# A chunk-by-chunk order for the first fresh tiles, and Newton steps on two columns at once

## The chip, the cores and the metric

The kernel runs on one core of a Trainium2 chip. Its time is the device time of one execution in microseconds (us); the number quoted is the median of three runs. A profile is one further execution with a hardware trace. TensorE (PE) multiplies matrices, VectorE (DVE) and ScalarE (ACT) work element by element, GpSimd (POOL) helps a little, and SyncE's queue (SP) loads weights from memory.

## What is computed

Two network blocks in a row, for 256 tokens of width 1024, in float32. The first block is an RMS norm, two recurrent mixers, and a mixture of 32 experts. The second block has two layers, each of which treats the tokens `h` and, beside them, 256 context tokens `hc`: a feed-forward, a mixer of two attentions and a Fourier branch, and a second feed-forward. The change touches the norms of both blocks and the feed-forwards and mixers of the second. Cut to these:

```python
def rmsnorm_2(x, g):
    return x * lax.rsqrt(jnp.mean(x * x, axis=-1, keepdims=True) + EPS) * g

def swiglu(x, wi, wo):
    g, u = jnp.split(x @ wi, 2, axis=-1)        # 1024 -> 2 x 2816
    return (jax.nn.silu(g) * u) @ wo            # 2816 -> 1024

def ffn_half(h, m, k, g_norm, wi, wo):
    hn = modulate(rmsnorm_2(h, g_norm), m[3 * k], m[3 * k + 1])   # * (1 + scale) + shift
    return h + 0.5 * m[3 * k + 2][:, None, :] * swiglu(hn, wi, wo)

for l in range(2):                              # second block
    h = ffn_half(h, ml, 0, ...); hc = ffn_half(hc, mc, 0, ...)
    hn = modulate(rmsnorm_2(h, norm_g[l, 1]), ml[3], ml[4])
    qa, ka, va, qb, kb, vb, uc, gl = project_tokens(hn, w_in[l], ...)
    h = h + ml[5][:, None, :] * merge_branches(ya, yb, yc, gl, ...)   # attentions and Fourier
    h = ffn_half(h, ml, 2, ...)
```

## The kernel before

Activations lie transposed: a tile of 128 features by 256 tokens, eight such chunks (k = 0 to 7) for the width of 1024. A product of full float32 quality is made of three matmuls (`mm3`, L327 to L329): both the weights and the activations are split in a high half (`whi`, `hnh`) and a low half (`wlo`, `hnl`), and high by high, low activation by high weight, and high activation by low weight are added up in one PSUM bank. So every output tile of 128 features costs 8 x 3 matmuls.

Weights come in pieces of 128 x 1024, that is eight 128 x 128 blocks. Class `_Stream` loads them in order, and splits each just before its first use: ScalarE writes `whi` (L312), VectorE subtracts and writes `wlo` (L313). There are three buffers for the halves in the second block, so piece c can be split only when TensorE has finished with piece c - 3. Here a piece is what one output tile needs: piece c holds the eight blocks of tile c.

Work is arranged in chains. Chain x is the first block's recurrent mixers, m the experts, c the context tokens, and z the main tokens in the second block; x, m and z follow each other, and c runs between x's and m's work, steered by a planner with estimated costs. A chain is a Python generator that issues instructions as it goes. TensorE and the SP queue keep the order in which the instructions were issued; on VectorE, ScalarE and GpSimd the framework's scheduler sets the order at build time, from its own estimates. On the chip every engine works its list off in that order, and a waiting instruction holds up all that stand behind it.

A norm goes like this (`rstd_cols`, L409): ones-matmuls (L421) leave the mean square of each token in a PSUM bank as two columns of 128 tokens; VectorE makes 1/sqrt of them by a bit trick (L423 to L426) and three Newton steps; two diagonal matrices `dg` (L442) and two matmuls (L443) spread the result over all partitions. Then `norm_split` writes the eight chunks of `hnh` and `hnl` (L456 to L462). The helper `rsqrt` (L342 to L344) makes the same Newton steps for the head norms with three instructions on all columns. There are 14 norms of the kind `rstd_cols`: x and m one each, c five, z seven.

In chain z the norms of the feed-forwards and mixers need not be awaited: `norm_early` runs the first six output tiles (pieces 0 to 5) on the raw activations `xs0`, `xs1`, and VectorE scales their results afterwards by `hnr` (L398, L399). These tiles are j < 3 of a feed-forward (each j is a gate tile and an up tile, two pieces) and j < 6 of a mixer. The first fresh tiles, which read `hnh` and `hnl`, come next: j = 3 of the feed-forward (pieces 6 and 7, in `up`, L1532) and j = 6 and 7 of the mixer (`project`, L1579). Chain c has no early tiles: its first fresh tiles are j = 0, and they already go chunk by chunk, so that a chunk of `hn` can be used as soon as it is there.

Of the kernel before, what the change touches and what calls it, by code (L numbers as in the profile page):

```python
# [15 lines left out]
OP = mybir.AluOpType  # L16
# [3 lines left out]
T = 256  # L20
D = 1024
KD = D // 128
# [201 lines left out]
class _Net:  # L224
# [184 lines left out]
    def rstd_cols(self, ch, x, w1=0.7, w2=2.2):  # L409

        nc, V = self.nc, self.nc.vector
        have = ch.top.acc is not None
        if not have:
            for k in range(KD):
                self.sumsq(ch, x[:, k], k, eng=V)
        acc, ch.top.acc = ch.top.acc, None
        yield 0.0, w1 if have else 5.0
        b = ch.bank()
        for i in range(2):
            for n, a in enumerate(acc):  # L420
                nc.tensor.matmul(b[:, i:i + 1], a[:, i * 128:i * 128 + 128], self.ones[:, :1], start=(n == 0), stop=(n == 1))  # L421
        v, a, y, t = (ch.tile([128, 2], f"rs{c}", bufs=2) for c in "vayt")
        V.tensor_scalar(v, b[:, :2], 1.0 / D, EPS, op0=OP.mult, op1=OP.add)  # L423
        V.tensor_scalar(t.bitcast(I32), v.bitcast(I32), 1, None, op0=OP.arith_shift_right)
        V.tensor_scalar(y.bitcast(I32), t.bitcast(I32), -1.0, float(0x5F3759DF), op0=OP.mult, op1=OP.add)
        V.tensor_scalar(a, v, -0.5, None, op0=OP.mult)  # L426
        c = [slice(i, i + 1) for i in range(2)]
        for _ in range(3):
            for i in c:
                V.scalar_tensor_tensor(t[:, i], y[:, i], a[:, i], y[:, i], op0=OP.mult, op1=OP.mult)  # L430
            for i in c:
                V.scalar_tensor_tensor(y[:, i], t[:, i], 1.5, y[:, i], op0=OP.add, op1=OP.mult)  # L432
        yield 0.5, w2
        return y

# [1082 lines left out]
    def ffn_body(self, ch, x, hn, gate, wi, wo, more, first, nxt):  # L1518
        nc = self.nc
        nh = JF // 2  # L1520

        def early(hi, lo, j):
            (g, gs), (u, us) = (self.scaled(ch, b, first[1]) for b in first[0][2 * j:2 * j + 2])
            nc.scalar.activation(g, g, AF.Identity, bias=gs)
            th = ch.tile([128, T], "w", bufs=ch.nw)
            nc.scalar.activation(th, g, AF.Tanh, scale=0.5)
            nc.vector.scalar_tensor_tensor(g, th, 1.0, g, op0=OP.add, op1=OP.mult)
            nc.vector.scalar_tensor_tensor(u, u, us, g, op0=OP.add, op1=OP.mult)
            nc.scalar.mul(hi, u, 0.5)
            nc.vector.scalar_tensor_tensor(lo, u, 0.5, hi.bitcast(F32), op0=OP.mult, op1=OP.subtract)  # L1530

        def up(p):  # L1532
            hh = ch.tile([128, nh, T], "h0", F32R, bufs=self.nh)
            hl = ch.tile([128, nh, T], "h1", F32R, bufs=self.nh)
            for jj in range(nh):
                j = p * nh + jj
                if first and j < 3:
                    early(hh[:, jj], hl[:, jj], j)
                    continue
                b = ch.bank()  # L1540
                order = [(h, k) for h in range(2) for k in range(KD)]
                for n, (h, k) in enumerate(sorted(order, key=lambda e: e[1]) if j == 0 else order):
                    if self.fine and n and n % 4 == 0:
                        yield 1.3
                    self.mm3(b[:, h * T:h * T + T], wi.get(j * 16 + h * 8 + k), (hn[0][:, k], hn[1][:, k]),
                             k == 0 and (h == 0 or j > 0), k == KD - 1, skip_group_check=(j == 0))
                th = ch.tile([128, T], "w", bufs=ch.nw)
                nc.scalar.activation(th, b[:, :T], AF.Tanh, scale=0.5)
                q = ch.tile([128, T], "w", bufs=ch.nw)
                nc.vector.scalar_tensor_tensor(q, th, 1.0, b[:, :T], op0=OP.add, op1=OP.mult)  # L1550
                hf = ch.tile([128, T], "w", bufs=ch.nw)
                nc.vector.scalar_tensor_tensor(hf, q, 0.5, b[:, T:], op0=OP.mult, op1=OP.mult)
                self.split_act(hh[:, jj], hl[:, jj], hf)
                yield 1.3 if self.fine else 5.2
            return hh, hl

        def down(p, h):
            for jo in range(KD):
                b = ch.bank()
                for k in range(nh):  # L1560
                    self.mm3(b[:, :T], wo.get(p * KD * nh + jo * nh + k), (h[0][:, k], h[1][:, k]), k == 0, k == nh - 1)
                nc.vector.scalar_tensor_tensor(x[:, jo], b[:, :T], gate[:, jo:jo + 1], x[:, jo],  # L1562
                                               op0=OP.mult, op1=OP.add)
                if p == 1 and more:
                    self.sumsq(ch, x[:, jo], jo, nxt)
                yield 3.6

        if self.nh == 2:
            h = []
            for p in range(2):  # L1570
                h.append((yield from up(p)))
            for p in range(2):
                yield from down(p, h[p])
        else:
            for p in range(2):
                h = yield from up(p)
                yield from down(p, h)

    def project(self, ch, hn, l, rope, y, w, first, full=True):  # L1579
# [8 lines left out]
        todo = list(range(18)) if full else [4, 5, 6, 7, 12, 13]  # L1588
        norm = [t for t in todo if t < 13]
        sb = ch.bank()  # L1590
        late = []
        for j in todo:
            if j == todo[0] and not first:
                two = [ch.bank() for _ in range(2)]
                for k in range(KD):
                    for n in range(2):
                        self.mm3(two[n][:, :T], w.get(todo[n] * 8 + k), (hn[0][:, k], hn[1][:, k]), k == 0, k == KD - 1)
            if first and j < 6:
                t, sft = self.scaled(ch, first[0][j], first[1])
                nc.scalar.activation(qk[:, j], t, AF.Identity, bias=sft)  # L1600
                b = qk[:, j]
            elif j in todo[:2]:
                b = two[todo.index(j)]
            else:
                b = ch.bank()
                for k in range(KD):
                    self.mm3(b[:, :T], w.get(j * 8 + k), (hn[0][:, k], hn[1][:, k]), k == 0, k == KD - 1)
            if len(late) == 3 or j > 12:
                for f in late:
                    f()  # L1610
                late = []
            if j < 13:
                sq = ch.tile([128, T], "w", bufs=ch.nw)
                nc.scalar.square(sq, b[:, :T])
                if not first or j >= 6:
                    nc.vector.tensor_copy(qk[:, j], b[:, :T])
                g = j % 4
                mine = [t for t in norm if t % 4 == g]
                late.append(partial(mm, sb[32 * g:32 * g + 32, :T], self.c("sel")[:, (j // 4) * 32:(j // 4) * 32 + 32],
                                    sq, start=(j == mine[0]), stop=(j == mine[-1])))  # L1620
                if j == norm[-1] and not full:
                    for f in late:
                        f()
                    late = []
                    rs = self.parted(ch, self.rsqrt(ch, sb[:, :T], T, EPS, tag="rw"))
            elif j == 13:
                if full:
                    rs = self.parted(ch, self.rsqrt(ch, sb[:, :T], T, EPS, tag="rw"))
                nc.vector.tensor_copy(vaT, b[:, :T])
            else:  # L1630
                lo, hi = uc[:, j - 14, :128], uc[:, j - 14, 128:]
                nc.scalar.copy(hi, b[:, 128:T])
                nc.vector.tensor_tensor(lo, b[:, :128], hi, op=OP.add)
                nc.vector.tensor_tensor(hi, b[:, :128], hi, op=OP.subtract)
            if not first or j >= 6:
                yield 2.7
        fill = _chain(self.values(ch, hn, w, vaT, r), self.fourier(ch, uc, y) if full else None)
        for c in self.rotate(ch, qk, norm, rs, l):
            yield c
            c = next(fill, None)  # L1640
# [552 lines left out]
```

## Time and profile before

| | us |
|---|---|
| median of three runs | 2859.76 (2856.36, 2860.39, 2859.76) |
| profiled execution, its own time | 2842.6 |
| its span from first to last instruction | 2840.8 |
| TensorE busy | 2700.0 |
| VectorE busy | 1781.4 |
| ScalarE busy | 1229.9 |

The profiled execution was 17 us shorter than the median of the runs, and its span is 1.8 us shorter than its own time. Main chain z fills the span from about 1541 us to the end; the first 1500 us hold the first block and the context chain. In the rows below, "x2" joins two instructions of one kind: the duration is then from the start of the first to the end of the second. A bracket at the end of a row is the idle time of that engine just before, and what ended it. A trailing letter in a name is the chain (bz, hnhz: chain z).

### The profile page before, as it was taken

How to read it: one execution, taken by the hardware profiler on the slowest of the kernel's cores; microseconds unless marked ns; L12 is line 12 of the kernel's file. 1: busy time of each engine (PE TensorE's matmuls, PEld its weight loads, DVE VectorE, ACT ScalarE, POOL GpSimd, SP SyncE). 2: the span in 40 equal slices, each digit the busy share in tenths (PEclk: the TensorE clock that was granted, in tenths of full speed). 3: DMA queues.
4: the chain of work that ended last, by engine and by line, in shares of the span. 5: the costliest groups of instructions: out<-in, count | busy, mean ns of one | idle time of the engine just before them, and what ended most of it. 6: DMA issues, size and time to landing. Idle time of an engine off the chain costs nothing. (4 is left out here: it accounts for less than half of the span.)

```text
span 2840.8 us, 59032 instructions
## 1 busy us (share of the span) xinstructions
PE 2700.0 (95%) x24390; PEld 2396.4 (84%) x24390; DVE 1781.4 (63%) x3501; ACT 1229.9 (43%) x2071; POOL 180.7 (6%) x187
## 2 busy tenths in 40 slices
PE   8998879999999999999997999999999999999999
PEld 6765568898677888888886999799999999799999
DVE  4776366455545554555456767777866767777765
ACT  4331143343344443334343545365544545465543
POOL 0110020000000200000000000101100000101100
PEclk9998979999999999999998999999999999999999
DMA  9857777887698889889794555434555555434553
GB/s 339 289 193 268 248 256 272 324 314 257 243 336 321 272 342 355 322 294 375 286 360 179 184 193 198 151 111 142 169 195 193 181 195 200 142 108 148 169 195 127
DMA packets 194562, 670.82 MB, mean 236 GB/s; under 512 B 29170, under 2 KB 33522, under 8 KB 193650
## 3 DMA queue, kind: packets, MB, share of 16 engines
q1 hardware_dynamic: 183856, 659.12, 65.6%
q10 hardware_dynamic: 10434, 7.90, 1.0%
q8 instruction: 192, 3.15, 0.4%
q14 instruction: 80, 0.66, 0.1%
HBM read 657.73 MB, written 5.80 MB: 234 GB/s over the span
## 5 line engine op out<-in xcount | busy, mean ns | idle before, releaser
L313 DVE TENSOR_TENSOR wlo<-raw,whi 128x1024 fp32r<-128x1024 f32 x631 | 775.5, 1230 | 513.1 <-ACT whi L312 499.4
L312 ACT CAST whi<-raw 128x1024 fp32r<-128x1024 f32 x639 | 670.9, 1050 | 763.4 <-issue 262.6
L327 PE MATMUL bz<-hnhz,whi 128*128 128x256 f32 x1920 | 541.8, 282 | 3.5 <-ACT whi L312 2.8
L329 PE MATMUL bz<-hnhz,wlo 128*128 128x256 f32 x1920 | 534.8, 279 | 7.0 <-DVE wlo L313 7.0
L328 PE MATMUL bz<-hnlz,whi 128*128 128x256 f32 x1920 | 534.9, 279 | 4.2 <-DVE hnlz L322 4.2
L327 PE MATMUL bc<-hnhc,whi 128*128 128x256 f32 x1504 | 434.0, 289 | 11.9 <-DMA raw<-win 7.1
L328 PE MATMUL bc<-hnlc,whi 128*128 128x256 f32 x1504 | 422.4, 281 | 6.4 <-DVE hnlc L462 4.7
L329 PE MATMUL bc<-hnhc,wlo 128*128 128x256 f32 x1504 | 421.3, 280 | 4.7 <-DVE wlo L313 4.7
L327 PEld LDWEIGHTS bz<-hnhz,whi 128*128 128x128 f32 x1920 | 363.6, 189 | 13.0 <-issue 6.1
L329 PEld LDWEIGHTS bz<-hnhz,wlo 128*128 128x128 f32 x1920 | 363.9, 190 | 7.7 <-DVE wlo L313 7.7
L328 PEld LDWEIGHTS bz<-hnlz,whi 128*128 128x128 f32 x1920 | 363.6, 189 | 5.5 <-DVE hnlz L322 5.4
L327 PEld LDWEIGHTS bc<-hnhc,whi 128*128 128x128 f32 x1504 | 286.2, 190 | 52.0 <-issue 28.7
L328 PEld LDWEIGHTS bc<-hnlc,whi 128*128 128x128 f32 x1504 | 285.8, 190 | 9.4 <-DVE hnlc L462 7.7
L329 PEld LDWEIGHTS bc<-hnhc,wlo 128*128 128x128 f32 x1504 | 285.7, 190 | 6.5 <-DVE wlo L313 6.5
L327 PE MATMUL bz<-h0z,whi 128*128 128x256 f32 x704 | 194.3, 276 | 0.0
L328 PE MATMUL bz<-h1z,whi 128*128 128x256 f32 x704 | 194.3, 276 | 0.0
L329 PE MATMUL bz<-h0z,wlo 128*128 128x256 f32 x704 | 194.3, 276 | 0.0
L327 PE MATMUL bc<-h0c,whi 128*128 128x256 f32 x528 | 151.4, 287 | 0.0
L328 PE MATMUL bc<-h1c,whi 128*128 128x256 f32 x528 | 146.9, 278 | 0.0
L329 PE MATMUL bc<-h0c,wlo 128*128 128x256 f32 x528 | 146.8, 278 | 0.0
L329 PEld LDWEIGHTS bz<-h0z,wlo 128*128 128x128 f32 x704 | 132.2, 188 | 0.0
L328 PEld LDWEIGHTS bz<-h1z,whi 128*128 128x128 f32 x704 | 132.2, 188 | 0.0
(698 smaller groups left out, 4992.0 us busy)
## 6 DMA issues: line engine op xcount, KB each, us to landing
raw<-wi SPq DMA_DIRECT2D x266, 512.0 KB, 4.7
raw<-moe_gu SPq DMA_DIRECT2D x177, 512.0 KB, 7.7
raw<-wada SPq DMA_DIRECT2D x144, 512.0 KB, 5.8
raw<-wo SPq DMA_DIRECT2D x129, 512.0 KB, 4.3
raw<-wbr SPq DMA_DIRECT2D x108, 512.0 KB, 4.1
raw<-win SPq DMA_DIRECT2D x104, 512.0 KB, 5.5
raw<-moe_dn SPq DMA_DIRECT2D x103, 512.0 KB, 6.8
room<-moe_gu SPq DMA_DIRECT2D x79, 512.0 KB, 9.2
```

What stands on the lines that cost most here:

```text
L312: self.nc.scalar.copy(hi, src)
L313: eng.tensor_tensor(lo, src, hi.bitcast(F32), op=OP.subtract)
L327: mm(out, w[0], x[0], start=first, stop=False, **kw)
L328: mm(out, w[0], x[1], start=False, stop=False, **kw)
L329: mm(out, w[1], x[0], start=False, stop=last, **kw)
```

## The change

Three edits. In `rstd_cols`, each Newton step was four instructions on single columns (two columns, each t = y*a*y and then y = (t + 1.5)*y); now it is three instructions on both columns (t = y*y, t = t*a, y = (t + 1.5)*y), as in `rsqrt`. In `up`, the chunk-by-chunk order was kept for j = 0; now it also holds for j = 3 where the first three were made early: for each k the gate block and the up block are used. In `project`, tiles 6 and 7 are now made together, chunk by chunk, where the first six were made early.

```diff
--- before.py
+++ after.py
@@ -424,12 +424,10 @@
         V.tensor_scalar(t.bitcast(I32), v.bitcast(I32), 1, None, op0=OP.arith_shift_right)
         V.tensor_scalar(y.bitcast(I32), t.bitcast(I32), -1.0, float(0x5F3759DF), op0=OP.mult, op1=OP.add)
         V.tensor_scalar(a, v, -0.5, None, op0=OP.mult)
-        c = [slice(i, i + 1) for i in range(2)]
         for _ in range(3):
-            for i in c:
-                V.scalar_tensor_tensor(t[:, i], y[:, i], a[:, i], y[:, i], op0=OP.mult, op1=OP.mult)
-            for i in c:
-                V.scalar_tensor_tensor(y[:, i], t[:, i], 1.5, y[:, i], op0=OP.add, op1=OP.mult)
+            V.tensor_tensor(t, y, y, op=OP.mult)
+            V.tensor_tensor(t, t, a, op=OP.mult)
+            V.scalar_tensor_tensor(y, t, 1.5, y, op0=OP.add, op1=OP.mult)
         yield 0.5, w2
         return y
 
@@ -1539,11 +1537,12 @@
                     continue
                 b = ch.bank()
                 order = [(h, k) for h in range(2) for k in range(KD)]
-                for n, (h, k) in enumerate(sorted(order, key=lambda e: e[1]) if j == 0 else order):
+                fresh = j == (3 if first else 0)
+                for n, (h, k) in enumerate(sorted(order, key=lambda e: e[1]) if fresh else order):
                     if self.fine and n and n % 4 == 0:
                         yield 1.3
                     self.mm3(b[:, h * T:h * T + T], wi.get(j * 16 + h * 8 + k), (hn[0][:, k], hn[1][:, k]),
-                             k == 0 and (h == 0 or j > 0), k == KD - 1, skip_group_check=(j == 0))
+                             k == 0 and (h == 0 or not fresh), k == KD - 1, skip_group_check=fresh)
                 th = ch.tile([128, T], "w", bufs=ch.nw)
                 nc.scalar.activation(th, b[:, :T], AF.Tanh, scale=0.5)
                 q = ch.tile([128, T], "w", bufs=ch.nw)
@@ -1589,18 +1588,19 @@
         norm = [t for t in todo if t < 13]
         sb = ch.bank()
         late = []
+        ahead = [6, 7] if first else todo[:2]
         for j in todo:
-            if j == todo[0] and not first:
+            if j == ahead[0]:
                 two = [ch.bank() for _ in range(2)]
                 for k in range(KD):
                     for n in range(2):
-                        self.mm3(two[n][:, :T], w.get(todo[n] * 8 + k), (hn[0][:, k], hn[1][:, k]), k == 0, k == KD - 1)
+                        self.mm3(two[n][:, :T], w.get(ahead[n] * 8 + k), (hn[0][:, k], hn[1][:, k]), k == 0, k == KD - 1)
             if first and j < 6:
                 t, sft = self.scaled(ch, first[0][j], first[1])
                 nc.scalar.activation(qk[:, j], t, AF.Identity, bias=sft)
                 b = qk[:, j]
-            elif j in todo[:2]:
-                b = two[todo.index(j)]
+            elif j in ahead:
+                b = two[ahead.index(j)]
             else:
                 b = ch.bank()
                 for k in range(KD):
```

First, TensorE at the first fresh tile of chain z's second feed-forward. The first row is k = 0. `whi_23967` is piece 6, before:

```order
L327 MATMUL bz_23964<-hnhz_23738,whi_23967 128x256
L328 MATMUL bz_23964<-hnlz_23739,whi_23967 128x256
L329 MATMUL bz_23964<-hnhz_23738,wlo_23968 128x256
L327 MATMUL bz_23964<-hnhz_23738,whi_23967 128x256
L328 MATMUL bz_23964<-hnlz_23739,whi_23967 128x256
L329 MATMUL bz_23964<-hnhz_23738,wlo_23968 128x256
```

and after, where `whi_23934` is piece 6 and `whi_23943` is piece 7:

```order
L327 MATMUL bz_23931<-hnhz_23705,whi_23934 128x256
L328 MATMUL bz_23931<-hnlz_23706,whi_23934 128x256
L329 MATMUL bz_23931<-hnhz_23705,wlo_23935 128x256
L327 MATMUL bz_23931<-hnhz_23705,whi_23943 128x256
L328 MATMUL bz_23931<-hnlz_23706,whi_23943 128x256
L329 MATMUL bz_23931<-hnhz_23705,wlo_23944 128x256
```

Before, all 24 matmuls on piece 6 came first, and piece 7 (`whi_23997`) followed. Now the sixth matmul needs `wlo` of piece 7, and pieces 6 and 7 are both in use until the tile's last chunk.

Second, VectorE at the same place, from `wlo` of piece 6 to `wlo` of piece 7, before:

```order
L313 TENSOR_TENSOR wlo_23968<-raw_23965,whi_23967 128x1024
L1527 SCALAR_TENSOR_TENSOR wz_23934<-wz_23943,wz_23934 128x256
L399 TENSOR_TENSOR wz_23949<-bz_23852,hnrz_23672 128x256
L1528 SCALAR_TENSOR_TENSOR wz_23938<-wz_23938,sftz_23939,wz_23934 128x256
L398 COPY sftz_23954<-bz_23883 128x1
L399 TENSOR_TENSOR wz_23953<-bz_23883,hnrz_23672 128x256
L313 TENSOR_TENSOR wlo_23998<-raw_23995,whi_23997 128x1024
```

and after:

```order
L313 TENSOR_TENSOR wlo_23935<-raw_23932,whi_23934 128x1024
L1525 SCALAR_TENSOR_TENSOR wz_23901<-wz_23910,wz_23901 128x256
L399 TENSOR_TENSOR wz_23916<-bz_23819,hnrz_23642 128x256
L1526 SCALAR_TENSOR_TENSOR wz_23905<-wz_23905,sftz_23906,wz_23901 128x256
L398 COPY sftz_23921<-bz_23850 128x1
L399 TENSOR_TENSOR wz_23920<-bz_23850,hnrz_23642 128x256
L313 TENSOR_TENSOR wlo_23944<-raw_23941,whi_23943 128x1024
```

The names are other numbers of the same buffers: nothing moved here. `wlo` of piece 7 still stands behind the scaling of early tile 5 (L399, reading the last early bank).

Third, VectorE at the plain norm with which chain z begins, where the context chain's last head norm (`wc`) is mixed in. From the last bit-trick instruction on, before:

```order
L425 TENSOR_SCALAR rsyz<-rstz 128x2
L343 TENSOR_TENSOR wc<-wc 128x256
L430 SCALAR_TENSOR_TENSOR rstz<-rsyz,rsaz 128x1
L344 SCALAR_TENSOR_TENSOR wc<-wc 128x256
L430 SCALAR_TENSOR_TENSOR rstz<-rsyz,rsaz 128x1
L342 TENSOR_TENSOR wc<-wc 128x256
L432 SCALAR_TENSOR_TENSOR rsyz<-rstz,rsyz 128x1 x2
L343 TENSOR_TENSOR wc<-wc 128x256
L430 SCALAR_TENSOR_TENSOR rstz<-rsyz,rsaz 128x1
L344 SCALAR_TENSOR_TENSOR wc<-wc 128x256
L430 SCALAR_TENSOR_TENSOR rstz<-rsyz,rsaz 128x1
L342 TENSOR_TENSOR wc<-wc 128x256
```

and after:

```order
L425 TENSOR_SCALAR rsyz<-rstz 128x2
L343 TENSOR_TENSOR wc<-wc 128x256
L428 TENSOR_TENSOR rstz<-rsyz 128x2
L344 SCALAR_TENSOR_TENSOR wc<-wc 128x256
L429 TENSOR_TENSOR rstz<-rstz,rsaz 128x2
L342 TENSOR_TENSOR wc<-wc 128x256
L430 SCALAR_TENSOR_TENSOR rsyz<-rstz,rsyz 128x2
L343 TENSOR_TENSOR wc<-wc 128x256
L428 TENSOR_TENSOR rstz<-rsyz 128x2
L313 TENSOR_TENSOR wlo<-raw,whi 128x1024
L344 SCALAR_TENSOR_TENSOR wc<-wc 128x256
L429 TENSOR_TENSOR rstz<-rstz,rsaz 128x2
```

Twelve Newton instructions became nine (six and five of them are in the rows shown). A `wlo` of the context chain, which before stood behind `dgz`, now stands in the second Newton step.

## Rows read from the trace of the kernel before

**Rows 1.** The page, part 1: busy us and share of TensorE.

```profile
PE 2700.0 (95%) x24390; PEld 2396.4 (84%) x24390; DVE 1781.4 (63%) x3501; ACT 1229.9 (43%) x2071; POOL 180.7 (6%) x187
```

**Rows 2.** Waits of TensorE, whole span: waited for: us, times, longest us.

```profile
PE bz L443 <- DVE dgz L442: 9.9, 9, 3.5
...
PE bz L329 <- DVE wlo L313: 7.0, 3, 2.6
...
PE bc L443 <- DVE dgc L442: 5.5, 4, 2.3
```

**Rows 3.** Timeline of VectorE, one norm (start us, duration us, instruction).

```profile
1571.16 0.35 DVE L430 SCALAR_TENSOR_TENSOR rstz<-rsyz,rsaz 128x1 f32<-128x1 f32 x2
...
1571.62 0.34 DVE L430 SCALAR_TENSOR_TENSOR rstz<-rsyz,rsaz 128x1 f32<-128x1 f32 x2
...
1572.53 0.47 DVE L442 TENSOR_SCALAR dgz<-const,rsyz 128x128 f32<-128x128 f32 x2
```

**Rows 4.** Timeline of VectorE, the head norms' helper.

```profile
912.85 0.17 DVE L342 TENSOR_TENSOR rbtc<-rbyc 128x8 f32<-128x8 f32 x1
...
913.45 0.17 DVE L342 TENSOR_TENSOR rbtc<-rbyc 128x8 f32<-128x8 f32 x1
```

**Rows 5.** Timeline of VectorE and TensorE, the norm before the first mixer.

```profile
1757.92 0.16 DVE L398 COPY sftz<-bz 128x1 f32<-128x1 f32 x1 [0.52 <-PE bz L329]
...
1758.51 0.48 DVE L442 TENSOR_SCALAR dgz<-const,rsyz 128x128 f32<-128x128 f32 x2
...
1758.85 0.71 PE L443 MATMUL bz<-dgz,const 128*128 128x128 f32 x4 [1.04 <-DVE dgz L442]
```

**Rows 6.** Timeline of VectorE, ScalarE, TensorE, the plain norm.

```profile
1543.17 0.43 DVE L343 TENSOR_TENSOR wc<-wc 128x256 f32<-128x256 f32 x1
...
1547.99 0.47 DVE L442 TENSOR_SCALAR dgz<-const,rsyz 128x128 f32<-128x128 f32 x2
...
1544.71 1.05 ACT L312 CAST whi<-raw 128x1024 fp32r<-128x1024 f32 x1 [4.51 <-PE bc L328]
...
1548.32 1.22 PE L443 MATMUL bz<-dgz,const 128*128 128x128 f32 x4 [3.52 <-DVE dgz L442]
```

**Rows 7.** Timeline, the main chain's second feed-forward: TensorE, VectorE, ScalarE.

```profile
2038.27 0.29 PE L327 MATMUL bz<-hnhz,whi 128*128 128x256 f32 x1
...
2038.85 0.28 PE L329 MATMUL bz<-hnhz,wlo 128*128 128x256 f32 x1
...
2036.60 1.21 DVE L313 TENSOR_TENSOR wlo<-raw,whi 128x1024 fp32r<-128x1024 f32 x1
...
2038.87 0.41 DVE L399 TENSOR_TENSOR wz<-bz,hnrz 128x256 f32<-128x256 f32 x1
2039.20 1.21 DVE L313 TENSOR_TENSOR wlo<-raw,whi 128x1024 fp32r<-128x1024 f32 x1
...
2035.73 1.04 ACT L312 CAST whi<-raw 128x1024 fp32r<-128x1024 f32 x1
...
2041.09 1.05 ACT L312 CAST whi<-raw 128x1024 fp32r<-128x1024 f32 x1 [0.52 <-PE bz L328]
```

**Rows 8.** Timeline, the main chain's first feed-forward: TensorE, VectorE.

```profile
1590.08 0.39 PE L329 MATMUL bz<-hnhz,wlo 128*128 128x256 f32 x1 [1.88 <-DVE wlo L313]
...
1588.81 1.22 DVE L313 TENSOR_TENSOR wlo<-raw,whi 128x1024 fp32r<-128x1024 f32 x1
...
1590.62 1.22 DVE L313 TENSOR_TENSOR wlo<-raw,whi 128x1024 fp32r<-128x1024 f32 x1
```

**Rows 9.** Timeline, the first mixer's first fresh tile: VectorE, TensorE.

```profile
1772.05 1.23 DVE L313 TENSOR_TENSOR wlo<-raw,whi 128x1024 fp32r<-128x1024 f32 x1
...
1774.42 0.38 PE L327 MATMUL bz<-hnhz,whi 128*128 128x256 f32 x1
```

**Rows 10.** Windows: stretch, length, TensorE busy (count), granted clock, DMA share, GB/s.

```profile
1590.00:1592.00 2.00, 1.92 (x16) 1.00 0.41 127
1995.00:1997.00 2.00, 1.85 (x8) 0.50 0.53 164
```

## The prediction

> **What bounds the kernel now.** I read the page's busy times first. TensorE is busy 2700 of 2840.8 us [rows 1], so the kernel is bound by TensorE and a change in time must come out of its 140 us of gaps, or add to them. Next I read what those gaps waited for [rows 2]. The `dg` matrices that follow the Newton steps account for 9.9 us in chain z and 5.5 in chain c; a part of the 9.9 (two of the nine waits) belongs to the attention's own norm, which the change leaves alone. Waits for `wlo` account for 7.0 us in z, in three waits. In z no fresh tile of a feed-forward or mixer waits for `hnh` or `hnl`: the view has no such row (the waits for `hnlz` there are all at L322, the mixer's output split). The six early tiles last long enough for all eight chunks of `hn` to be ready when the first fresh tile starts. So the wait that a chunk-by-chunk order could shorten is not there, and I looked instead at what the new orders make TensorE need sooner. After 1541 us z's TensorE has nothing else to do in a gap, so what it waits there moves the end by the same amount.
>
> **Newton steps.** Before, the steps of one norm start at 1571.16 and `dg` starts at 1572.53: 1.37 us for 12 instructions, 0.46 us per step (the second step starts at 1571.62) [rows 3]. Two instructions on separate columns overlap: a pair lasts 0.35 us from its first start to its last end, yet a step of two such pairs takes 0.46 us and not 0.70. The new form is one chain: each of the three needs the one just before. The helper for the head norms has this form on 8 columns, and there a step of three instructions takes 913.45 - 912.85 = 0.60 us, 0.20 us for each [rows 4]. So nine of them take 1.80 us and the norm becomes 0.43 us longer, though it issues fewer instructions. Bounds from the rows: if an instruction cost what it does on average before (1.37/12 = 0.114 us), nine would take 1.03 us, 0.34 less than before; if each took as long as a pair does now, half of 0.46, they would take 2.07, 0.70 more. I take 0.20, since that row is the same operations in the same dependence, and only 6 columns wider.
>
> The Trainium skill speaks against this. Its page "VectorE: DVE Perf Modes" says under "Rules for kernel authors" that chained VectorE operations should be reduced in number, since each empties the pipeline whether or not the next needs it. By that rule three instructions fewer would make each norm shorter; the trace doesn't agree, as independent pairs overlap (0.35 us for two) and dependent ones stand 0.20 apart. The other result is the first rival below.
>
> Where does it count? After nearly every one of the 14 norms TensorE runs out of work and waits for `dg` (in the experts' norm for the router's input), as in the row of 1.04 us [rows 5]; so I count every delay of the steps in full. Nine norms at 0.43 us make 3.9 us. In four norms of z a copy of a shift (`sft`) cuts the steps in two and waits for TensorE's first early tile. In the row shown it starts at 1757.92 and `dg` follows at 1758.51, 0.59 us later [rows 5]. Now five steps of 0.20 us stand behind the copy (0.07 us), so `dg` follows 1.07 us after it: 0.48 us more, 1.9 us for the four. A fifth norm has the same pattern and counts among the nine; so do norms in x, c and m where a few foreign instructions fill the gaps of the chain or go ahead of its end, with deviations both ways that I let cancel.
>
> The fourteenth is the plain norm with which z begins. Its steps are mixed with a head norm of c, so gaps are filled and fewer instructions give nothing: 12 short ones in six single and three paired places become nine single ones. But `wlo`, which stood behind `dg`, now stands in the second step. VectorE would come to it about 1545.0 (8 of the some 21 instructions between 1543.17 and 1547.99 in front of it). It needs `whi`, which ScalarE starts at 1544.71 behind TensorE and ends at 1545.76, a wait of 0.7 us. Then come its own 1.2 us (the duration of such a split in [rows 7]). So `dg` starts about 1.9 us later, and TensorE, which already waits 3.52 us there [rows 6], waits 5.4. Below: 0, if the split came through as early as VectorE is free and something else there is faster; above 2.6. Its old place behind `dg` was hidden behind TensorE's spreading, so nothing comes back.
>
> Newton steps together: 3.9 + 1.9 + 1.9 = 7.7 us longer. From the bounds (thirteen norms at -0.34 or +0.70 and the plain norm at 0 or 2.6) this goes from -4.4 to +11.7.
>
> **The first fresh tile of z's feed-forwards.** Here the order of TensorE changes and that of VectorE in front of the tile doesn't, in three of the four feed-forwards (the second to the fourth). In the second, the tile starts at 2038.27. VectorE has started `wlo` of piece 6 at 2036.60, ahead of time, but that of piece 7 only at 2039.20, behind the scaling of the last early tile; it ends 1.21 us later, at 2040.41 [rows 7]. Before, piece 7 was needed only 24 matmuls later and nobody waited. Now the sixth matmul needs it. That one stood at 2038.85; it can go 0.05 us after the split's end (a split that ended at 1588.81 + 1.22 = 1590.03 released its matmul at 1590.08 [rows 8]), at 2040.46. TensorE waits 1.61 us that it didn't wait before. ScalarE's `whi` of piece 7 is not the cause: it was cast from 2035.73 to 2036.77. The third and fourth feed-forwards show the same distances within 0.02 us: 3 x 1.6 = 4.8 us. Both the tile's start and the split hang on `dg`, so the longer norm shifts them alike. Bounds: 0 if the split started when `whi` was there (2036.77 + 1.21 = 2037.98, before it is needed), 2.1 (the whole distance from the tile's start to the split's end) above.
>
> Queued behind the waiting matmul is all of TensorE. Pieces 6 and 7 are now both released only at the tile's end, some 2040.5 + 4.9 = 2045.4 (43 matmuls at 0.115), where before ScalarE could cast piece 9 at 2041.09, when piece 6 was released [rows 7]. Piece 8 has the third buffer and keeps TensorE busy for 24 x 0.115 = 2.8 us; casting and splitting piece 9 takes 1.05 + 1.21 us. That is 0.5 us of slack, so I cost it at nothing; if the cover fails it is up to 1 us per place.
>
> In the first feed-forward VectorE is late already: TensorE waits 1.88 us for `wlo` of piece 6, and that of piece 7 runs from 1590.62 to 1591.84 [rows 8]. There the new order puts the rest of `hn` ahead of the scaling, and two short instructions fewer stand before piece 7's split, so it ends about 1591.2, needed at about 1588.4. The wait becomes some 2.6 instead of 2.0 us: +0.6, between 0 and +1.4 (1591.84 + 0.05 - 1588.4 - 2.0).
>
> **The mixers.** There `wlo` of piece 7 has ended at 1773.28, more than a microsecond before the first fresh tile at 1774.42 [rows 9]. Nothing was waited for and nothing will be: 0. The late release of pieces 6 and 7 has the cover of piece 8 here too, with ScalarE's two squares in front of the casts: 0 to 0.5 us each.
>
> **Sum.** 7.7 + 4.8 + 0.6 = 13.1 us. The profiled execution took 2842.6 us and would take 2855.7. The median of the runs lies 17 us higher; I add the same 13.1 to it: 2859.8 + 13.1 = 2872.9 us, 0.46% slower.
>
> **Rivals.** (1) Not slower: VectorE costs by the number of instructions, dependent or not. Place: the steps of all 14 norms; price: 14 x 0.34 = 4.8 us less instead of 7.7 more. With the new waits for piece 7 (5.4) that is 2860.4, no change. It decides where a chained instruction takes less than 1.37/9 = 0.15 us. Against it stands the 0.20 of [rows 4]; for it, that only 8 columns were seen and not 2. Were the splits early enough as well, it would be 2855, and with the 1.88 us of the first feed-forward saved, 2853, faster. (2) The delays are absorbed: the norms of x, c and m (seven at 0.43, 3.0 us) disappear in the planner's slack and in a wait for a weight load, and half of the rest too: 2860 + 5 = 2865, at the edge of no change. For it: chain c runs beside the experts' work, and DMA is busy then; against it: TensorE waits in these norms as well [rows 2]. (3) The clock: after z's waits in the first mixer's output the granted clock is 0.50 (the level of 1.2 GHz) for 1995 to 1997, while after the single wait of 1.88 us it is 1.00 (2.4 GHz) for 1590 to 1592 [rows 10]. The new waits of 1.6 us are shorter than the one that left it, but the longer waits at `dg` and the two in the first feed-forward could tip it. At half clock 2 us do the work of one; some 3.8 us of that in each of three to five places is +6 to +9 us: about 2880.
>
> **How the numbers follow.** The forecast has 0.65, the clock 0.16, the absorbed delays 0.12, the count of instructions 0.07. A change of 0.2% (5.7 us) is about what a measurement of this kernel can tell from none. The forecast's own range is 2866 to 2878. The range for 8 in 10 goes down to 2862, into the absorbed cases, and up to 2882, with the clock's. Slower by over 0.2% means above 2865.5: the forecast and the clock, and a little of the rest, 0.84. Within 0.2%: 0.12. Faster by more: 0.04.
>
> **What would show it.** In the new profile, Newton instructions at 0.20 us from start to start, `dg` waits in z summing to 4 to 6 us more, and a wait of some 1.6 us for `wlo` at the sixth matmul of the first fresh tile in feed-forwards two to four. The mixers show no new wait. If the chained instructions stand 0.12 apart, or `wlo` of piece 7 is ready before the tile starts, I am wrong.

## The result, and the profile after

The changed kernel takes 2870.6 us (median of 8 runs) where the kernel before takes 2857.6 (8 runs, the three quoted above among them): 12.9 us more, against a forecast of 13.1. The ratio estimated from all runs is 1.0055 (of the two medians alone 1.0045), with a 95% interval of 1.0036 to 1.0074, that is 10 to 21 us. The profiled execution took 2861.65 us and its span is 2859.8, which is 19.0 more than before. TensorE's busy time went from 2700.0 [rows 1] to 2707.5 us.

The waits of TensorE over the whole span (what waited, for what: us, times, longest us). Code lines behind the norms are two lower in the changed kernel: L441 is L443 of before, L440 is L442.

```profile
PE bz L441 <- DVE dgz L440: 14.3, 9, 5.3
PE bz L329 <- DVE wlo L313: 11.4, 7, 2.6
...
PE bc L441 <- DVE dgc L440: 7.2, 4, 2.8
...
PE bm L1133 <- DVE rt1m L1155: 3.7, 1, 3.7
```

Against [rows 2], z waits 4.4 us more for `dg`, 4.4 more for `wlo` (seven waits in place of three), and c waits 1.7 more for `dg`. The experts' wait for their router's input (the last row) was 3.4 us before, and x's waits for `dg` went from 1.2 to 1.4. There is no new row for the mixers.

The Newton steps of the norm shown in [rows 3], on VectorE (start us, duration us, instruction):

```profile
1580.77 0.16 DVE L428 TENSOR_TENSOR rstz<-rsyz 128x2 f32<-128x2 f32 x1
1580.96 0.16 DVE L429 TENSOR_TENSOR rstz<-rstz,rsaz 128x2 f32<-128x2 f32 x1
1581.16 0.16 DVE L430 SCALAR_TENSOR_TENSOR rsyz<-rstz,rsyz 128x2 f32<-128x2 f32 x1
1581.36 0.16 DVE L428 TENSOR_TENSOR rstz<-rsyz 128x2 f32<-128x2 f32 x1
...
1582.53 0.28 DVE L440 TENSOR_SCALAR dgz<-const,rsyz 128x128 f32<-128x128 f32 x1
```

They stand 0.195 us apart, and from the first to `dg` 1.76 us pass, where before it was 1.37: 0.39 more, with three instructions fewer.

Before the first mixer, where the copy of a shift cuts the steps in two (VectorE; [rows 5] before):

```profile
1768.57 0.16 DVE L398 COPY sftz<-bz 128x1 f32<-128x1 f32 x1 [1.01 <-PE bz L329]
1768.65 0.15 DVE L429 TENSOR_TENSOR rstz<-rstz,rsaz 128x2 f32<-128x2 f32 x1
...
1769.62 0.29 DVE L440 TENSOR_SCALAR dgz<-const,rsyz 128x128 f32<-128x128 f32 x1
```

From the copy to `dg` it is 1.05 us (1.07 forecast, 0.59 before). The wait of TensorE behind it is now 1.84 us instead of 1.04.

The plain norm with which z begins, on VectorE ([rows 6] before):

```profile
1554.34 0.15 DVE L428 TENSOR_TENSOR rstz<-rsyz 128x2 f32<-128x2 f32 x1
1555.17 1.22 DVE L313 TENSOR_TENSOR wlo<-raw,whi 128x1024 fp32r<-128x1024 f32 x1 [0.67 <-ACT whi L312]
...
1556.64 0.15 DVE L429 TENSOR_TENSOR rstz<-rstz,rsaz 128x2 f32<-128x2 f32 x1
...
1559.14 0.47 DVE L440 TENSOR_SCALAR dgz<-const,rsyz 128x128 f32<-128x128 f32 x2
```

The split stands inside the second step, waits 0.67 us for `whi` and takes 1.22, as worked out. TensorE's wait at this `dg` is 5.31 us, against 3.52: 1.8 more.

The second feed-forward of z on TensorE, and the split that it waits for on VectorE ([rows 7] before):

```profile
2053.59 0.39 PE L329 MATMUL bz<-hnhz,wlo 128*128 128x256 f32 x1 [1.44 <-DVE wlo L313]
```

```profile
2051.99 0.41 DVE L399 TENSOR_TENSOR wz<-bz,hnrz 128x256 f32<-128x256 f32 x1
2052.32 1.21 DVE L313 TENSOR_TENSOR wlo<-raw,whi 128x1024 fp32r<-128x1024 f32 x1
```

The split ends at 2053.53, behind the scaling (L399) of the last early tile, and the sixth matmul starts 0.06 us later. The third and fourth feed-forward have the same wait of 1.45 us. In the first, the one wait of 1.88 us [rows 8] became two, for pieces 6 and 7:

```profile
1598.77 0.39 PE L329 MATMUL bz<-hnhz,wlo 128*128 128x256 f32 x1 [0.56 <-DVE wlo L313]
...
1600.70 0.39 PE L329 MATMUL bz<-hnhz,wlo 128*128 128x256 f32 x1 [1.31 <-DVE wlo L313]
```

That is 1.87 us together, no more than before.

How the 19.0 us of the two profiles divide: to the plain norm's spreading matmuls at z's start the changed kernel needs 11.2 us more (1559.48 against 1548.32 [rows 6]), and from there to the end 7.8. The rows of the windows (stretch, length, busy time and count of TensorE, weight loads, VectorE, ScalarE, GpSimd, then granted clock, DMA share, GB/s), after and before:

```profile
1559.48:2859.80 1300.32, 1255.58 (x10549) 1208.45 (x10549) 909.66 (x1550) 668.12 (x1119) 88.65 (x74) 0.99 0.49 165
```

```profile
1548.32:2840.80 1292.48, 1255.33 (x10549) 1208.34 (x10549) 911.62 (x1569) 668.49 (x1119) 89.23 (x74) 0.99 0.49 166
```

Of the 11.2 in front, the waits named above make 4.0 (1.7 in c, 0.2 in x, 0.3 in m, 1.8 at the plain norm). Much of the rest is clock: up to that place the mean granted clock is 0.96, and 0.97 before, and the changed kernel's profile has short stretches at half clock where the first profile of before has none. One of them, after and before (x's second norm):

```profile
124.00:127.00 3.00, 2.68 (x12) 2.68 (x13) 3.00 (x7) 0.75 (x1) 0.00 (x0) 0.50 0.93 326
```

```profile
119.00:126.00 7.00, 5.26 (x45) 3.79 (x46) 7.00 (x14) 2.10 (x3) 0.59 (x2) 1.00 0.86 300
```

The experiments show that such stretches come and go between executions of one program.

### The profile page after: what moved, and what is told of

Its sections match the earlier page's. It is cut to its first block, busy times and chain, and to the rows that moved or that the text cites. A ratio compares the mean times of both kernels' runs of the same rounds, so it can differ in the third digit from the quotient of the medians.

```text
span 2859.8 us, 58986 instructions
## 1 busy us (share of the span) xinstructions
PE 2707.5 (95%) x24390; PEld 2406.5 (84%) x24390; DVE 1779.8 (62%) x3459; ACT 1229.5 (43%) x2071; POOL 180.2 (6%) x187
## 5 line engine op out<-in xcount | busy, mean ns | idle before, releaser
L329 PEld LDWEIGHTS bz<-hnhz,wlo 128*128 128x128 f32 x1920 | 364.0, 190 | 12.9 <-DVE wlo L313 12.9
L327 PEld LDWEIGHTS bz<-h0z,whi 128*128 128x128 f32 x704 | 132.2, 188 | 0.0
```

The lines of the kernel that those rows point to most:

```text
L327: mm(out, w[0], x[0], start=first, stop=False, **kw)
L329: mm(out, w[1], x[0], start=False, stop=last, **kw)
```

## The experiments

Theory of the forecast: dependent Newton instructions cost about 0.20 us each and nearly all of it is on the path; the feed-forward order adds a wait for piece 7's `wlo`; the mixers' order is free. Rivals: VectorE costs by the count of instructions; the delays are absorbed; the clock drops behind the new waits. The first four kernels were timed beside 32 runs of the kernel before (2856.2 us median, 2845.6 to 2866.1).

**1. The Newton steps alone.**

```
-            for i in c: V.scalar_tensor_tensor(t[:, i], y[:, i], a[:, i], y[:, i], ...)
-            for i in c: V.scalar_tensor_tensor(y[:, i], t[:, i], 1.5, y[:, i], ...)
+            V.tensor_tensor(t, y, y, op=OP.mult)
+            V.tensor_tensor(t, t, a, op=OP.mult)
+            V.scalar_tensor_tensor(y, t, 1.5, y, op0=OP.add, op1=OP.mult)
```

> The kernel before with one part of the change: the Newton steps on both columns at once, nothing else. Theory (the steps are a chain; 0.20 us from one instruction to the next against 0.46 us for a step of two overlapping pairs before): 7.7 us longer than before, ratio 1.0027, with Newton instructions 0.19 to 0.20 us apart and z's waits for dg 4 to 5 us more, 1.9 of it in the plain norm. Rival (VectorE costs by the number of instructions): 4.8 us shorter, ratio 0.998, with them under 0.15 us apart. Rival (absorbed): within 2 us of before.

Measured: 2867.2 us, ratio 1.0043 [1.0026, 1.0060]. TensorE's waits, whole span:

```profile
PE bz L441 <- DVE dgz L440: 14.3, 9, 5.3
...
PE bc L441 <- DVE dgc L440: 7.2, 4, 2.8
...
PE bz L329 <- DVE wlo L313: 5.8, 3, 2.6
```

The `dg` waits are those of the full change, so they are all the Newton steps'. Both rivals of this run are out: fewer instructions did not make the norms shorter, and the delays were not absorbed. The last row is a gain that was not forecast: the first feed-forward waits 0.57 us for `wlo` and not 1.88 [rows 8].

```profile
1604.40 0.39 PE L329 MATMUL bz<-hnhz,wlo 128*128 128x256 f32 x1 [0.57 <-DVE wlo L313]
```

The ratio stands for some 12 us, more than these waits (6.1 more for `dg`, 1.2 less for `wlo`: 4.9). The rest goes with the clock: the mean granted clock of its 12 timed executions is 0.970, of the 32 runs of before 0.972. Time multiplied by clock, a rough measure of the work at full clock, averages 2780.4 us against 2775.6: 4.8 more, what the waits add up to.

**2. The feed-forward order alone.**

```
-  ... enumerate(sorted(order, key=lambda e: e[1]) if j == 0 else order):
+  fresh = j == (3 if first else 0)
+  ... enumerate(sorted(order, key=lambda e: e[1]) if fresh else order):
```

> The kernel before with one part of the change: the chunk-by-chunk order of the first fresh tile of the feed-forwards. Theory (the sixth matmul now needs wlo of piece 7, whose split stands behind the scaling of the last early tile): three new waits of 1.4 to 1.6 us in z's second to fourth feed-forward and 0 to 0.6 in the first, 4.3 to 5.4 us longer, ratio 1.0015 to 1.0019. Rival (absorbed: the weight-loading of later pieces had a wait that this one replaces): no change. Rival (clock): the new waits tip the granted clock to 0.50 behind them, 9 us or more, ratio 1.003 and up.

Measured: 2869.7 us, ratio 1.0055 [1.0037, 1.0073], three times what was expected. The profile has the waits as expected, 5.6 us more than in [rows 2]; the `dg` waits are unchanged:

```profile
PE bz L329 <- DVE wlo L313: 12.6, 7, 2.6
PE bz L443 <- DVE dgz L442: 9.9, 9, 3.5
```

From the plain norm to the end it took 1301.3 us, 8.8 more than before. But that was the shortest of nine executions; the longest is 25 us above it, at a mean clock of 0.972 against 0.975. Time multiplied by clock puts four of the nine at 2783 to 2788 us and five at 2797 to 2802; the 32 runs of before reach from 2769 to 2781. So there is a second cost that comes and goes and is not the clock; run 7 shows what it may be. Of the 8.8, the first feed-forward has 3.1: 1.2 of wait (1.87 and then 1.19, before 1.88), and a clock drop behind it:

```profile
1595.00:1599.00 4.00, 4.00 (x23) 4.00 (x23) 1.39 (x3) 0.28 (x1) 0.00 (x0) 0.57 0.71 243
```

Four us at 0.57 lose 1.7.

**3. The mixers' order alone.**

```
+  ahead = [6, 7] if first else todo[:2]
-  if j == todo[0] and not first:
+  if j == ahead[0]:
```

> The kernel before with one part of the change: in the mixers with early tiles the two fresh tiles 6 and 7 go chunk by chunk. Theory: no new wait, ratio 1.000 (0 to +1 us, from the later release of two weight pieces). It also shows what the granted clock does from one run of practically the same work to the next: theory of the clock as run-to-run noise: means between 0.969 and 0.978, and stretches at 0.50 ahead of 1500 us that are not the same from one execution to the next.

Measured: 2852.9 us, ratio 0.9984 [0.9966, 1.0001]: no cost, and no new wait for `wlo` in z:

```profile
PE bz L329 <- DVE wlo L313: 6.9, 3, 2.6
```

The profiled execution, at a mean clock of 0.967, reached the plain norm at 1570.0, where the same program until there took 1548.3 before; behind it, it needed 1292.3 us, the same as before within 0.2.

**4. Two Newton steps in place of three**, on separate columns.

```
-  for _ in range(3):
+  for g in (1.5008789, 1.5000006):     # in place of 1.5; first guess 0x5F376908
```

> The kernel before with two Newton steps in place of three in the 14 norms, on separate columns as before; first guess and the two constants (1.5008789 and 1.5000006 for 1.5) are set so that the result is still within 8e-7 of the square root's inverse. Prices a step directly. Theory (nearly every norm is on the path): 14 x 0.46 = 6.4 us shorter, ratio 0.9978. Rival (the steps lie beside other work or in slack, so the waits for dg are ended by something else): under 2 us, ratio over 0.9993; then the Newton term of the prediction would be wrong too.

Measured: 2844.4 us, ratio 0.9962 [0.9945, 0.9978], 11.8 us less than before. The waits for `dg` shrink by 4.5 in z and 3.3 in c:

```profile
PE bz L443 <- DVE dgz L442: 5.4, 8, 1.9
...
PE bc L443 <- DVE dgc L442: 2.2, 3, 0.9
```

So a step in front of `dg` is paid at least in full, in both directions. The theory's 6.4 us lie at the edge of the interval (6 to 16 us). Two norms gave more than the 0.46 us of a step. The wait at z's plain norm, whose steps are mixed with other work, fell from 3.52 to 1.87; one in c fell from 2.35 to 0.46, because a split (`wlo`, 1.22 us) that stood in front of its last Newton instruction now stands behind `dg`.

**5. Nine instructions with a shorter chain.** (This run and 6 and 8 beside 29 runs of before, 2855.7 us.)

```
+  V.tensor_tensor(t, y, y, op=OP.mult); V.tensor_tensor(a, t, a, op=OP.mult)     # r in a
+  for n in range(3):
+      if n < 2: V.scalar_tensor_tensor(t, a, 1.5, a, op0=OP.add, op1=OP.mult)
+      V.scalar_tensor_tensor(y, a, 1.5, y, op0=OP.add, op1=OP.mult)
+      if n < 2: V.scalar_tensor_tensor(a, a, 1.5, t, op0=OP.add, op1=OP.mult)
```

> The kernel before with Newton steps on both columns at once, nine instructions as in the change and the same result up to rounding, but written so that only seven of them form the chain: r = a*y*y is carried along (r(1.5+r)^2), and y(1.5+r) stands beside it. Theory (dependent instructions stand 0.195 us apart, an independent one costs 0.08 or hides): 7 x 0.195 = 1.37 us from the first step to dg, the same as before; z's waits for dg back to 10 to 12 us, time within 3 us of before, ratio 0.999 to 1.001. Rival (it is the number of instructions, or the two-column form itself, that costs): 9 x 0.195 = 1.76 us and the same time as the kernel with the change's Newton steps alone, ratio about 1.004.

Measured: 2861.2 us, ratio 1.0014 [0.9996, 1.0033]; z waits 12.3 us for `dg`, between 9.9 and 14.3. On VectorE, in c:

```profile
1521.88 0.16 DVE L427 TENSOR_TENSOR rstc<-rsyc 128x2 f32<-128x2 f32 x1
...
1522.27 0.16 DVE L431 SCALAR_TENSOR_TENSOR rstc<-rsac 128x2 f32<-128x2 f32 x1
1522.35 0.15 DVE L432 SCALAR_TENSOR_TENSOR rsyc<-rsac,rsyc 128x2 f32<-128x2 f32 x1
1522.54 0.16 DVE L434 SCALAR_TENSOR_TENSOR rsac<-rsac,rstc 128x2 f32<-128x2 f32 x1
...
1523.39 0.29 DVE L444 TENSOR_SCALAR dgc<-const,rsyc 128x128 f32<-128x128 f32 x1
```

Same number, same shape, 1.51 us in place of 1.76: it is the chain that counts. The theory's 1.37 was 0.14 short, because an independent instruction is not quite free: it starts 0.08 behind its neighbour, and the next dependent one stands 0.19 behind the independent one, not behind the one it takes its operand from. (It also overwrites what the independent one reads, so these rows don't tell which of the two holds it.)

**6. The second half six chunks later.**

```
-  sorted(order, key=lambda e: e[1])
+  sorted(order, key=lambda e: e[1] + 6 * e[0])
```

> The kernel before with the fresh feed-forward tile chunk by chunk, but its second half (piece 7) six chunks behind its first (piece 6), so that wlo of piece 7 is needed at the 24th matmul, 2.6 us after the tile's start, and not at the sixth. Theory (the loss is the wait for that split, which is ready 2.2 us after the start): the three waits of 1.45 us and the 1.2 us of the first feed-forward vanish, ratio 1.000 (0 to +2 us). Rival (the chunk-by-chunk order itself costs, by the late release of two weight pieces at once): no wait at the sixth matmul, but the loss stays at 4 us and more, ratio 1.002 and up, with waits for whi or wlo at later pieces.

Measured: 2857.8 us, ratio 1.0001 [0.9983, 1.0019]. The waits are back to three:

```profile
PE bz L329 <- DVE wlo L313: 6.8, 3, 2.6
```

So the loss lies in when piece 7's split is needed, and not in the mixing of two pieces as such. The late release of the pieces isn't tested here: in this order TensorE is done with piece 6 after 27 of the tile's 48 matmuls (24 before, 45 with the change). Against it speaks run 2, where z's waits for `whi` are those of before (2.8 us, two waits) and no later piece has a new wait for `wlo`. This run's profile took 2864.5 us; in its first feed-forward (193.9 us, 186.0 before) it has the slow matmuls that run 7 shows, and 1.7 us lost at half clock.

**7. The feed-forward order once more, for a second profile.**

> The kernel with the feed-forward part alone once more, for a second profile: its timed runs spread from 2854 to 2879 us, and the profiled one was the shortest. Theory (the spread is the clock ahead of 1500 us and at single places): from z's plain norm to the end again 1301 us, 9 us more than before, the rest of the difference in stretches at clock 0.50. Rival (the part has a second cost that comes and goes, in z): over 1305 us from the plain norm to the end, with waits that the first profile does not have.

Measured: 2873.6 us; from the plain norm to the end 1312.2 us, 20 more than before. The waits are those of run 2 (12.4 us for `wlo`). But z's third and fourth feed-forward lasted 191.9 us where run 2 had 185.6. Windows of the same length in the second and third feed-forward of this execution:

```profile
2055.50:2219.50 164.00, 163.45 (x1443) 163.36 (x1443) 107.58 (x145) 80.30 (x115) 6.81 (x6) 1.00 0.59 193
2241.50:2405.50 164.00, 164.00 (x1395) 164.00 (x1394) 103.08 (x139) 76.70 (x109) 6.06 (x5) 1.00 0.57 184
```

The clock is 1.00 in both and TensorE is never idle in the second, yet it does 1395 matmuls and not 1443: 0.1176 us each in place of 0.1133. So the rival was right that a second cost comes and goes, and wrong that it is a wait.

**8. The best of both.** Two steps, with the mixers' order.

> Two Newton steps in place of three (as in the run with two steps), with the change's chunk-by-chunk order in the mixers and not in the feed-forwards. Theory (additive: the steps' gain and nothing for the mixers): ratio 0.996, about 2845 us; below the kernel before and the changed one. Rival (the mixers' order gains as well): ratio 0.994 to 0.995.

Measured: 2843.7 us, ratio 0.9961 [0.9942, 0.9980]. It is faster than both kernels; the mixers' order adds nothing to run 4.

**9 to 12. Second and third profiles**, for the count of such slow feed-forwards; one execution each.

> The changed kernel once more, for a second profile. In a profile of the feed-forward part alone two of z's four feed-forwards ran their matmuls 0.1176 us apart in place of 0.1133 from the new wait to the end of the stream, 6.2 us longer each, without a further wait. Theory (the changed order can leave the stream in the slower spacing): 0 to 2 of the four feed-forwards at 0.118, each 6 us longer than 186; the waits as in its first profile, z's dg 14.3 and wlo 11.4 us. Rival (that was a single disturbed execution): all four at 0.113.

> The changed kernel a third time, for the same count. Theory: over this and the run before it, one to three of eight feed-forwards at 0.118 us a matmul. Rival: none.

> The kernel before with the feed-forward order alone, a third profile. Its timed runs, multiplied by their clock, fall into two groups some 13 us apart, which would be two feed-forwards at the slower spacing. Theory: zero, two or more of the four feed-forwards at 0.118, and the time from the plain norm to the end 1301 us plus 6.2 for each of them. Rival: all at 0.113, 1301 us.

> The kernel before itself, a second profile. Theory: all four of z's feed-forwards at 0.113 us a matmul, 1292 to 1295 us from the plain norm to the end; what differs from its first profile is the clock ahead of 1550 us. Rival (the slower spacing has nothing to do with the order): one or two of them at 0.118 here too.

Measured: run 9 2862.1 us and run 10 2876.2 (the changed kernel), run 11 2867.4 (the feed-forward order alone), run 12 2855.7 (before). The `dg` and `wlo` waits of z repeat within 0.1 us. Slow feed-forwards: none in 9 and 11, z's first in 10 and, against the theory, in 12 (its row):

```profile
1599.00:1763.00 164.00, 164.00 (x1394) 164.00 (x1394) 103.87 (x139) 76.68 (x109) 6.05 (x5) 1.00 0.56 185
```

So the change's order is not needed for it. Over all 14 profiles: of 32 feed-forwards in which TensorE restarts behind a wait for `wlo` (the first one of z in every kernel, the others only with the change's order) 5 ran at 0.1176 (the first in runs 6, 10 and 12, two in run 7); of 24 without such a wait none. That fits a cost of restarting behind the wait, but 5 cases are few, and no run shows what decides.

## Why the prediction was right, point by point

| step | forecast, us | rows of the runs, us |
|---|---|---|
| Newton steps in x, m, c | 3.0 | 2.2 |
| plain norm | 1.9 | 1.8 |
| from there to the end: norms 2.8, feed-forwards 4.8 and 0.6, mixers 0 | 8.2 | 7.8 (7.6 in run 9; 11.9 in run 10, with a slow feed-forward) |
| sum | 13.1 | 11.8 |
| medians | 13.1 | 12.9 |

The mechanism was right: the chain, the plain norm's split and the early need of piece 7 came where they were forecast, each within 0.2 us. That the sums agree so closely is in part luck. The interval of the measured difference is 10 to 21 us. Of the 7.8, longer waits for `dg` and `wlo` make 7.0; a gain of some 2 us at the clock (below) and some 3 us that these waits don't cover nearly cancel. The 7.8 also sets two profiles without slow feed-forwards against each other; run 12, the kernel before with one, took 1299.1 us there, 6.5 more than the first profile.

- **Newton steps.** 0.20 us apart from the head norms' row [rows 4], and measured 0.195; 0.39 more per norm (0.43 forecast). The waits for `dg` after one feed-forward or mixer rose by 0.38 to 0.46 each, with two exceptions: 0.80 in front of the first mixer, where the wait also begins 0.34 us earlier against the copy (at 1768.12 with the copy at 1768.57; before at 1757.81 and 1757.92), and 0.15 in the feed-forward where it was already 1.34. In x, m and c 2.2 came of 3.0: behind c's first norm TensorE waits no longer than before (2.39 and 2.40 us), and in x only 0.2 longer. The first rival doesn't hold: twelve instructions took 1.37 (before), nine 1.76 (the changed kernel), nine others 1.51 (run 5). The rule of the Trainium skill, "VectorE: DVE Perf Modes", section "Rules for kernel authors", to minimize the count of chained operations does not hold for these instructions either.
- **Plain norm.** The split's place, its wait of 0.7 and the 1.8 us came as worked out. The sentence that nothing comes back was wrong in most executions. The next 24.55 us of before took 23.39 in the changed kernel, in spite of 1.0 us of additional waits in them: before, the clock fell a second time in that stretch. That second fall stands in five of the seven profiles with the old three steps; the other two, runs 6 and 11, took 23.0 and 22.8 us. In the four with the change's steps it is missing, and the stretch takes 23.4 us in each. Its mean clock is 0.80 before and 0.89 after:

```profile
1548.32:1572.87 24.55, 22.30 (x92) 17.13 (x92) 16.67 (x44) 11.85 (x24) 4.76 (x6) 0.80 0.42 140
```

```profile
1559.48:1582.87 23.39, 20.13 (x91) 15.52 (x91) 15.32 (x40) 12.25 (x24) 4.77 (x6) 0.89 0.37 124
```

- **First fresh tile, feed-forwards 2 to 4.** 1.61 us forecast, 1.45 measured each (4.35 for 4.8), for the reason given; run 6 shows it by taking most of the early need away. Each of these feed-forwards becomes 1.7 to 1.8 us longer in run 2, a little more than its wait.
- **First feed-forward.** 0.6 forecast, 0 in the full change (two waits of 1.87 in place of one of 1.88), 1.2 with the order alone (1.87 and then 1.19). The difference is the gain of run 1, which the forecast did not see. The forecast's own sum is also off: by its figures the wait becomes 2.85 us (1591.2 + 0.05 - 1588.4), 0.85 more than its 2.0 and not 0.6, and its bound is 1.5 and not 1.4.
- **Mixers, and the cover of piece 9.** No new waits, as forecast; run 3 bears the zero out for the mixers, and the waits for `whi` in run 2 for the feed-forwards.
- **The clock.** The third rival put drops behind the new waits. In z's first feed-forward all three profiles of the feed-forward order alone (runs 2, 7, 11) have 1.7 us of drop, at waits of 1.87 and 1.19 us. But runs 4 and 6 have it as well, at the one wait of 1.88 us that the kernel before has, and the other four profiles with that one wait (before, 3, 8, 12) don't. So a new wait is not needed for it, though it may make it likelier. The changed kernel (1.31 us at most there, three profiles) and runs 1 (0.57) and 5 (1.08) have none. The forecast's 3.8 us at half clock per place, 1.9 of them lost, stand in no row; where a drop came it lost 1.7. Behind the new waits of feed-forwards 2 to 4 no profile has one. But half-clock stretches do decide what one execution takes. Six profiles with the same program up to z (before and runs 2, 3, 7, 11, 12) reached the plain norm's `dg` between 1548.3 (before) and 1570.0 (run 3); the four with the Newton steps between 1559.5 and 1570.0. The means are 1558.3 and 1563.7, 5.4 apart where 4.9 was forecast; with such a scatter this is weak support, and the sum of waits is the better measure.

What stays open: each part alone moved the time by more than its rows (12 and 16 us by the ratios, 4.9 and 8.8 by rows), and together they moved it 16, not 28. For the feed-forward order the slow restarts of run 7 could fill the gap: the upper group of its timed runs lies 13 us above the lower, the price of two. But only one of the nine has a trace, from the lower group and without a slow feed-forward, so that isn't shown, nor why the changed kernel, with as many waits, has only one of eight runs that far up. For the Newton steps it is the lower mean clock, and whether the order of the instructions brings that about or chance does was not settled.

## What to carry to other kernels

Before fusing tiny operations, count the length of the dependence chain and not the instructions: two interleaved chains on half the data beat one chain on all of it, and a shorter chain (here one Newton step fewer with better constants) beats both. Before advancing a consumer by reordering its work, look at what the new order needs first, and where the producer of that stands in its engine's queue. Compare executions by the waits and by stretches between the same two places; totals of one execution can differ by 20 us for the same program.

## What the runs showed of the hardware that was not expected

A stream of 128x256 matmuls with a weight load each has two spacings at a granted clock of 1.00: 0.1133 and 0.1176 us. It keeps the one in which it starts behind a wait until the end of the feed-forward, some 165 us on, and the slower costs 6.3 us there (191.9 in run 7 against 185.6 in run 2). What decides between them is not known.

In the first 1550 us, stretches at the half clock come at different places from one execution to the next of the same program; its time up to z's first norm differed by up to 22 us in six profiles.
